# Attention scores as float32 products of 64 rows, two heads in the two row halves

## The chip, the cores and the metric

The kernel runs on one core of a Trainium2 chip. The metric is the device time of one execution in microseconds (us). The engines are TensorE (PE in the rows, PEld for its weight loads), VectorE (DVE), ScalarE (ACT), GpSimd (POOL) and SyncE (SP), which issues most of the DMAs.

## What is computed

A batch of one sequence of 512 tokens goes through two blocks in float32. The first block has two layers, each a hybrid mixer and a SwiGLU feed-forward. The mixer holds three kinds of heads side by side: attention with a sliding window, hgrn (a gated recurrence in chunks) and gdn (a delta rule in chunks). The second block has an even layer (attention over 512 own and 256 context tokens beside a two-directional mLSTM), a mixture of experts, an odd layer of window means, and again a mixture of experts. The scores of the two attentions are what the change is about:

```python
def sliding_window_attention(q, k, v, sinks):       # 8 query heads, 2 key heads of 64
    ...
    scores = jnp.einsum('bnqhgd,bnkhd->bnhgqk', qb, kb).astype(jnp.float32) * (d ** -0.5)
    ...                                             # 128 queries against 256 keys at a time
    m = jnp.maximum(scores.max(axis=-1, keepdims=True), sink)
    p = jnp.exp(scores - m)
...
def attend_blocks(q, k, v):                         # 8 query heads, 2 key heads, 768 keys
    ...
        s = jnp.einsum('bhgtd,bhsd->bhgts', qblk, kt).astype(jnp.float32) * scale
        p = jax.nn.softmax(s, axis=-1).astype(vt.dtype)
        return jnp.einsum('bhgts,bhsd->bhgtd', p, vt)
```

Four query heads share one key head. A head has 64 elements, so a score product sums over 64 rows of an array that has 128.

## The kernel before

All of it is one program on one core. The stages follow each other: layer 0 (stage "a0", then its feed-forward), layer 1, the even layer (stage "b"), experts, odd layer, experts. In a stage, pieces of work are written as Python generators that `mix` and `track` interleave; the order in which instructions then stand on each engine is set by a scheduler that runs over a simulated timeline (L2229). Tiles come from rotating pools, so a buffer's reuse is a wait. PSUM has eight banks of 128 x 512 float32, divided by name: in the layers two each for "pd", "pg", "po" and "ph", in the even stage two "pd", one "po", one "pn" and four "pe".

**Layers.** gdn is `gen_gdn` (banks "pg"), hgrn `gen_hgrn` (banks "ph"), attention `gen_attn` (L1251, banks "pd" and "po"). Queries ("aq", in the even stage "eqt") and keys and values ("kv") are projected with tokens in the partitions, normalized per head and rotated (the rope). To be multiplied, a head must be turned so that its 64 elements lie in the partitions. `stacked` (L1236) does that for one head, for each of four blocks of 128 tokens with two instructions: a transpose (`tr`) into rows 0 to 63 of a bank and a float32 product with the identity (`mm`) into rows 64 to 127. A float32 product appears as two records on TensorE.

`qstack` (L1244) turns that bank into a stack: ScalarE rounds it to the type F32R, GpSimd copies the rounded upper half, and DVE subtracts the rounded lower half from the exact one. So one stack holds a head's rounded queries in rows 0 to 63 and the rest in rows 64 to 127. Keys are split in the same way into a rounded part and a rest (`split`), each in both halves. One head's scores are then two F32R products of 128 rows, with the rounded keys and with their rest:

```python
                    self.mm(p[:, hh, k0:], Q, KS[:, h // 4, 0, K], True, False)
                    self.mm(p[:, hh, k0:], Q, KS[:, h // 4, 1, K], False, True)
```

In the layers `scores` goes over four blocks of 128 queries and four head pairs. A head pair shares one "pd" bank, DVE adds the mask and takes the maximum, ScalarE takes Exp into "sm". `gen_values` then transposes the weights (into "pg", from there to "PT") and multiplies with the values into "po"; the next block's scores run beside it.

**Even stage** (`even`, L1522). The same with `kstack` (L1389) for 512 own keys and 256 context keys (KSc, made early, between the input projections). `stack` inside it runs behind `rope`, beside the mLSTM (banks "pe", output projection through "pn"). In `scores` a head pair's own scores take two "pe" banks and its context scores, both heads side by side, one more. DVE reduces each of the three banks to its maximum, ScalarE takes four Exps ("eP"). "X" is the name of all large tiles (four buffers, `big`): hidden states, query stacks and key stacks.

Of the kernel before, what the change touches and what calls it, by code (L numbers as in the profile page):

```python
# [9 lines left out]
F32 = mybir.dt.float32  # L10
F32R = mybir.dt.float32r
I32 = mybir.dt.int32
AF = mybir.ActivationFunctionType
# [155 lines left out]
class Net:  # L169
# [1065 lines left out]

    def stacked(self, src, nb, tag="pd"):  # L1236

        p = self.psm(tag)
        for b in range(nb):
            self.tr(p[0:64, b * 128:b * 128 + 128], src(b))  # L1240
            self.mm(p[64:128, b * 128:b * 128 + 128], src(b), self.C("ident"))
        return p[:, :nb * 128]

    def qstack(self, QS, p):  # L1244

        tmp = self.t([128, 512], "qtmp", F32R)
        self.act(tmp, p)
        self.nc.gpsimd.tensor_copy(QS[0:64], tmp[0:64].bitcast(F32))
        self.tt(QS[64:128], p[64:128], tmp[64:128].bitcast(F32), OP.subtract)

    def gen_attn(self, l, qts, kv, out, banks):  # L1251
# [18 lines left out]
        for b in range(4):  # L1270
# [25 lines left out]
        def scores(b, keys):  # L1296
            k0 = 0 if b else 128
            K = slice(b * 128 - 128 + k0, b * 128 + 128)
            nm, den = self.t([128, 8], "nm"), self.t([128, 8], "den")
            P = []  # L1300
            for h2 in range(4):
                p = self.psm("pd").rearrange("p (h s) -> p h s", h=2)
                sm = self.t([128, 2, 256], "sm")
                hs = slice(2 * h2, 2 * h2 + 2)
                for hh in range(2):
                    h = 2 * h2 + hh
                    Q = QS[h // 4][:, h % 4, b * 128:b * 128 + 128]
                    self.mm(p[:, hh, k0:], Q, KS[:, h // 4, 0, K], True, False)
                    self.mm(p[:, hh, k0:], Q, KS[:, h // 4, 1, K], False, True)
                    nc.vector.tensor_tensor_reduce(sm[:, hh, k0:], p[:, hh, k0:], self.C("amask")[:, k0:], 1.0,  # L1310
                                                   self.P(f"sink{l}")[:, h:h + 1], OP.add, OP.max, nm[:, h:h + 1])
                self.ts(nm[:, hs], nm[:, hs], -1.0, OP.mult)
                for hh in range(2):
                    h = 2 * h2 + hh
                    x = sm[:, hh, k0:]
                    self.act(x, x, AF.Exp, bias=nm[:, h:h + 1], accum_out=den[:, h:h + 1])
                    P.append(sm[:, hh])
                yield
# [70 lines left out]
    def kstack(self, KS, kv, nb):  # L1389
        for i in range(2):  # L1390
            p = self.stacked(lambda b: kv[:, b, i * 64:i * 64 + 64], nb, "pd")
            self.split(p, KS[:, i, 0], KS[:, i, 1])

# [128 lines left out]
    def even(self, X, Xc, out, project):  # L1522
# [70 lines left out]

        stacks = []

        def rope():
# [15 lines left out]

        def stack():
            KS = self.big([128, 2, 2, 512], F32R)
            self.kstack(KS, kv, 4)
            yield
            QS = [self.big([128, 4, 512], F32R) for i in range(2)]
            stacks.extend([KS, QS])
            for h in range(8):
                self.qstack(QS[h // 4][:, h % 4], self.stacked(lambda b: qt[:, b, h * 64:h * 64 + 64], 4))  # L1620
                yield

        A = lambda g: self.track(g, "A", "pd")
        pk()
        self.run(pq(0), pq(1), silu(0), silu(1))
        self.run(self.mix((chain(ml(0), ml(2)), 1), (chain(iter([0, 0]), ml(1), ml(3)), 1), (chain(po(0), po(1), A(chain(pa(0), pa(1), rope(), stack()))), 3)))
        self.grp, self.pg = "A", "pd"
        KS, QS = stacks
        ao = [self.t([128, 512], "ao", grp="E") for j in range(4)]
        def scores(b, keys):  # L1630
            nm, den = self.t([128, 8], "nm"), self.t([128, 2, 8], "den")
            P, Pc = [], []
            for h2 in range(4):
                G = h2 // 2
                m3 = self.t([128, 2, 2], "em3")
                Q = [QS[G][:, (2 * h2 + hh) % 4, b * 128:b * 128 + 128] for hh in range(2)]
                pc = self.psm("pe").rearrange("p (h s) -> p h s", h=2)
                pl = []
                for hh in range(2):
# [5 lines left out]
                for hh in range(2):  # L1645
                    self.mm(pc[:, hh], Q[hh], self.KSc[:, G, 0], True, False)
                    self.mm(pc[:, hh], Q[hh], self.KSc[:, G, 1], False, True)
                nc.vector.tensor_reduce(m3[:, 1], pc, AX.X, OP.max)
                hs = slice(2 * h2, 2 * h2 + 2)
                self.tt(nm[:, hs], m3[:, 0], m3[:, 1], OP.max)  # L1650
                self.ts(nm[:, hs], nm[:, hs], -1.0, OP.mult)
                for hh in range(2):
                    h = 2 * h2 + hh
                    P.append(self.t([128, 512], "eP", grp="E"))
                    Pc.append(self.t([128, 256], "eP", grp="E"))
                    self.act(P[h], pl[hh], AF.Exp, bias=nm[:, h:h + 1], accum_out=den[:, 0, h:h + 1])
                    self.act(Pc[h], pc[:, hh], AF.Exp, bias=nm[:, h:h + 1], accum_out=den[:, 1, h:h + 1])
                yield
# [393 lines left out]
def build(nc, tc, a, cwhere, pwhere):  # L2052
    with ExitStack() as ctx:
# [20 lines left out]
        for l in range(2):  # L2074
            with ExitStack() as st:
                n.open(st, f"a{l}", {"G0": 11, "G1": 4, "G2": 20, "P2": 8, "I0": 1, "I1": 1, "I2": 8, "A0": 6, "A1": 3, "A2": 10, "B2": 2},
                       {"pd": 2, "pg": 2, "po": 2, "ph": 2})
# [70 lines left out]
        with ExitStack() as st:  # L2148
# [6 lines left out]
            m = n.m  # L2155
            n.KSc = m.tile([128, 2, 2, 256], F32R, name="KSc")
            n.V = m.tile([128, 6, 128], F32, name="V")
# [75 lines left out]
```

## Time and profile before

| | us |
|---|---|
| median of 3 runs | 3138.05 |
| lowest, highest | 3137.93, 3151.81 |
| the profiled execution | 3138.86 |
| its span, first to last instruction | 3137.1 |
| TensorE busy | 2956.0 (94%) |
| DVE busy | 1442.7 (46%) |
| ScalarE busy | 896.7 (29%) |
| GpSimd busy | 375.9 (12%) |
| mean share of the DMA engines | 56% (q1) |

The profile is one execution. Its chain view begins at the last instruction and goes back from each piece of work to what released it, so its shares tell which engine's work set the end. A window view gives for a stretch of time how long each engine was busy in it, the mean clock that TensorE was granted (1.00 is 2.4 GHz, 0.5 is 1.2 GHz) and what the DMA engines did. A timeline lists the records of one engine, like neighbours joined into one row with their count. A TensorE record's own length overlaps the next one's start, since products are pipelined; what a group takes from the engine is the distance from its start to the next group's start.

### The profile page before, as it was taken

To read this page: it belongs to the slowest core of one execution; us is meant where nothing else is said; L and a number is where in the kernel's file an instruction comes from. 1 tells how busy PE (TensorE), PEld (TensorE's weight loads), DVE (VectorE), ACT (ScalarE), POOL (GpSimd) and SP (SyncE) were. 2 spreads that over 40 slices of the span, in tenths; PEclk is the share of its full clock that TensorE was granted. 3 is DMA by queue.
4 is the path that set the end of the run, shared out by engine and by line. 5 is a ranking of instruction groups with operands and counts; after the bars stand their busy time and mean duration, and the time that the engine had idled before them with its cause. 6 is when DMAs were issued, how large, how long until landed. Compare 5 with 4: busy or idle time off the path is not lost.

```text
span 3137.1 us, 42862 instructions
## 1 busy us (share of the span) xinstructions
PE 2956.0 (94%) x17699; PEld 1982.9 (63%) x17699; DVE 1442.7 (46%) x2704; ACT 896.7 (29%) x1714; POOL 375.9 (12%) x308
## 2 busy tenths in 40 slices
PE   7999899999999899999999899899999988999998
PEld 5875678888886667888898855534444384344343
DVE  4345766564546658689545654411211362111112
ACT  4332443233432344423344434301101122011011
POOL 0212211011023202213100310100000021000000
PEclk9996899999999699999999989899999998999998
DMA  6233146563220016599512100699999828999995
GB/s 216 68 135 106 35 143 181 176 188 88 90 68 12 1 58 209 149 293 313 151 57 68 34 14 14 252 405 409 409 409 409 312 82 342 409 390 397 407 409 214
DMA packets 334403, 637.02 MB, mean 203 GB/s; under 512 B 16640, under 2 KB 204288, under 8 KB 334208
## 3 DMA queue, kind: packets, MB, share of 16 engines
q1 hardware_dynamic: 332128, 634.15, 55.9%
q8 instruction: 139, 2.28, 0.3%
q10 hardware_dynamic: 2080, 0.13, 0.0%
q14 instruction: 56, 0.46, 0.0%
HBM read 632.14 MB, written 2.10 MB: 202 GB/s over the span
## 4 chain that ended last, share of the span: by engine, by line
PE 85%; DVE 9%; ACT 2%; DMA 2%; issue 1%; POOL 0%; SPq 0%; DVEq 0%; POOLq 0%; ACTq 0%
PE pd L297 41%; PE pm L297 18%; PE pa L297 8%; PE po L297 4%; PE pg L297 4%; PE pe L297 3%; PE pd L301 3%; PE ph L297 2%; DVE aacc L294 1%; PE pn L297 1%; DVE x L294 1%; DMA raw<-ada_w 1%; PE pg L301 1%; DVE split L285 1%; DVE rt L285 1%
## 5 line engine op out<-in xcount | busy, mean ns | idle before, releaser
L297 PE MATMUL pd<-X,split 128*128 128x512 f32 x2640 | 629.7, 394 | 11.5 <-ACT X L274 6.8
L297 PEld LDWEIGHTS pd<-X,split 128*128 128x128 f32 x2640 | 493.2, 189 | 121.6 <-ACT X L274 10.0
L297 PE MATMUL pm<-rawx,xs 128*64 128x512 f32 x1440 | 403.7, 602 | 0.9 <-ACT xs L274 0.5
L297 PEld LDWEIGHTS pm<-rawx,xs 128*64 128x64 f32 x1440 | 126.2, 137 | 191.1 <-issue 181.9
L297 PE MATMUL pa<-rawx,maT 128*64 128x512 f32 x728 | 203.1, 601 | 7.6 <-ACT maT L274 7.6
L274 ACT ACTIVATE split<-raw 128x1024 fp32r<-128x1024 f32 (+5 forms) x164 | 142.0, 871 | 194.9 <-PE pd L297 130.9
L285 DVE TENSOR_TENSOR split<-raw,split 128x1024 fp32r<-128x1024 f32 (+4 forms) x135 | 150.5, 1120 | 89.5 <-ACT split L274 88.8
L297 PE MATMUL pd<-split,X 128*128 128x256 f32 x1296 | 179.0, 292 | 9.5 <-ACT split L274 5.8
L297 PEld LDWEIGHTS pd<-split,X 128*128 128x128 f32 x1296 | 164.6, 195 | 16.1 <-ACT split L274 5.9
L297 PE MATMUL pd<-X,splitx 128*128 128x512 f32 x720 | 173.6, 391 | 0.0
L297 PEld LDWEIGHTS pd<-X,splitx 128*128 128x128 f32 x720 | 135.6, 189 | 29.3
L297 PE MATMUL pd<-aH,split 128*128 128x512 f32 x484 | 153.4, 389 | 0.0
L294 DVE SCALAR_TENSOR_TENSOR x<-pd,modl,x 128x512 f32<-128x512 f32 x136 | 96.6, 746 | 98.1 <-PE pd L297 98.0
L294 DVE SCALAR_TENSOR_TENSOR yL<-pa,gv,yH 128x512 fp32r<-128x512 f32 x32 | 24.0, 751 | 245.9 <-ACT yH L274 245.9
L297 PEld LDWEIGHTS pa<-rawx,maT 128*64 128x64 f32 x728 | 67.4, 137 | 107.5 <-issue 95.9
L1985 DVE COPY gv<-pd 64x1 f32<-64x1 f32 x32 | 5.0, 156 | 273.8 <-PE pd L297 273.5
L285 DVE TENSOR_TENSOR ms<-ms,pm 128x512 f32<-128x512 f32 x32 | 22.0, 688 | 226.9 <-issue 186.9
L294 DVE SCALAR_TENSOR_TENSOR aacc<-rawx,cs_c,aacc 128x512 f32<-128x512 f32 x148 | 125.4, 889 | 0.0
L285 POOL TENSOR_TENSOR aL<-sg,aH 128x512 fp32r<-128x512 f32 x44 | 66.9, 1520 | 399.6 <-ACT aH L274 399.6
L297 PEld LDWEIGHTS pd<-aH,split 128*128 128x128 f32 x484 | 90.9, 188 | 19.3
L274 ACT ACTIVATE split<-rawx 128x1024 fp32r<-128x1024 f32 (+3 forms) x64 | 59.6, 934 | 151.6 <-PE pd L297 126.2
L297 PE MATMUL pm<-raw,xs 128*64 128x512 f32 x272 | 101.5, 597 | 0.0
(694 smaller groups left out, 4868.3 us busy)
## 6 DMA issues: line engine op xcount, KB each, us to landing
rawx<-w_exp_gate SPq DMA_DIRECT2D x94, 1024.0 KB, 15.9
rawx<-w_exp_down SPq DMA_DIRECT2D x91, 1024.0 KB, 12.5
rawx<-w_exp_up SPq DMA_DIRECT2D x86, 1024.0 KB, 18.0
raw<-ada_w SPq DMA_DIRECT2D x30, 1024.0 KB, 5.4
rawx<-w_mod SPq DMA_DIRECT2D x29, 1024.0 KB, 5.7
raw<-w_in SPq DMA_DIRECT2D x22, 1024.0 KB, 5.1
raw<-w_exp_up SPq DMA_DIRECT2D x20, 1024.0 KB, 16.9
raw<-w_mod SPq DMA_DIRECT2D x19, 1024.0 KB, 5.8
```

The costliest lines, as they stand in the source:

```text
L274: i = self.nc.scalar.activation(out, in_, f, **k)
L285: return (eng or self.nc.vector).tensor_tensor(out, a, b, op)
L294: return self.nc.vector.scalar_tensor_tensor(out, a, s, b, op0, op1)
L297: return self.nc.tensor.matmul(out, l, r, start=start, stop=stop, skip_group_check=True)
L301: return self.nc.tensor.transpose(out, x, self.C("ident")[0:k, 0:k])
L1985: nc.vector.tensor_copy(gv[64 * i:64 * i + 64], pg[64 * i:64 * i + 64, i:i + 1])
```

## The change

The stacks go. Instead of one head per transposition, two neighbouring heads (128 columns of the projected queries) are transposed at once: `gen_heads` makes four groups of four transposes, each 128 x 128, and ScalarE copies each group to a tile QT, head 2m in rows 0 to 63 and head 2m+1 in rows 64 to 127. For the keys, `twice` first has ScalarE copy each key head twice side by side ("kk"), so that the transposed key head (KT) lies in both halves. A head's scores are then one plain float32 product of 64 rows; the two heads of a pair are issued one after the other, from the two row halves and into two different banks.

In the layers this holds both "pd" banks for two head pairs. In the even stage a head pair takes all four "pe" banks, two for the own and two for the context scores, and DVE reduces four pieces instead of three. Rounding, the copies on GpSimd and the subtractions on DVE fall away, and KSc is half as large. The pool "A1" of the layers gets a fourth buffer.

```diff
-    def stacked(self, src, nb, tag="pd"):
-
-        p = self.psm(tag)
+    def twice(self, kv, nb, KT, tag="pd"):
+
+        kk = []
         for b in range(nb):
-            self.tr(p[0:64, b * 128:b * 128 + 128], src(b))
-            self.mm(p[64:128, b * 128:b * 128 + 128], src(b), self.C("ident"))
-        return p[:, :nb * 128]
-
-    def qstack(self, QS, p):
-
-        tmp = self.t([128, 512], "qtmp", F32R)
-        self.act(tmp, p)
-        self.nc.gpsimd.tensor_copy(QS[0:64], tmp[0:64].bitcast(F32))
-        self.tt(QS[64:128], p[64:128], tmp[64:128].bitcast(F32), OP.subtract)
+            t = self.t([128, 2, 2, 64], "kk")
+            self.act(t, self.bc1(kv[:, b, 0:128].rearrange("p (h e) -> p h e", h=2), 2))
+            kk.append(t.rearrange("p h i e -> p h (i e)"))
+        for i in range(2):
+            p = self.psm(tag)
+            for b in range(nb):
+                self.tr(p[:, b * 128:b * 128 + 128], kk[b][:, i])
+            self.act(KT[:, i], p[:, :nb * 128])
+            yield
+
+    def gen_heads(self, qt, kv, nb, tag="pd"):
+
+        QT, KT = self.big([128, 4, 512]), self.big([128, 2, 512])
+        self.stacks = KT, QT
+        yield from self.twice(kv, nb, KT, tag)
+        for m in range(4):
+            p = self.psm(tag)
+            for b in range(4):
+                self.tr(p[:, b * 128:b * 128 + 128], qt[:, b, m * 128:m * 128 + 128])
+            self.act(QT[:, m], p)
+            yield
...
-        KS = self.big([128, 2, 2, 512], F32R)
-        for i in range(2):
-            p = self.stacked(lambda b: kv[:, b, i * 64:i * 64 + 64], 4)
-            self.split(p, KS[:, i, 0], KS[:, i, 1])
-            yield
-        QS = [self.big([128, 4, 512], F32R) for i in range(2)]
-        for h in range(8):
-            self.qstack(QS[h // 4][:, h % 4], self.stacked(lambda b: qt[:, b, h * 64:h * 64 + 64], 4))
-            yield
+        yield from self.gen_heads(qt, kv, 4)
+        KT, QT = self.stacks
...
-            for h2 in range(4):
-                p = self.psm("pd").rearrange("p (h s) -> p h s", h=2)
...
-                    self.mm(p[:, hh, k0:], Q, KS[:, h // 4, 0, K], True, False)
-                    self.mm(p[:, hh, k0:], Q, KS[:, h // 4, 1, K], False, True)
...
+            for G in range(2):
+
+                pp = [self.psm("pd").rearrange("p (m s) -> p m s", m=2) for hh in range(2)]
+                for m in range(2):
+                    sm = self.t([128, 2, 256], "sm")
+                    h2 = 2 * G + m
+                    hs = slice(2 * h2, 2 * h2 + 2)
+                    for hh in range(2):
+                        r = slice(hh * 64, hh * 64 + 64)
+                        self.mm(pp[hh][:, m, k0:], QT[r, h2, b * 128:b * 128 + 128], KT[r, G, K])
...
-        self.kstack(self.KSc, Pair(kv.t[4:]), 2)
+        self.run(self.twice(Pair(kv.t[4:]), 2, self.KSc))
...
-                pc = self.psm("pe").rearrange("p (h s) -> p h s", h=2)
-                pl = []
-                for hh in range(2):
-                    p = self.psm("pe")
-                    self.mm(p, Q[hh], KS[:, G, 0], True, False)
-                    self.mm(p, Q[hh], KS[:, G, 1], False, True)
-                    nc.vector.tensor_reduce(m3[:, 0, hh:hh + 1], p, AX.X, OP.max)
-                    pl.append(p)
-                for hh in range(2):
-                    self.mm(pc[:, hh], Q[hh], self.KSc[:, G, 0], True, False)
-                    self.mm(pc[:, hh], Q[hh], self.KSc[:, G, 1], False, True)
-                nc.vector.tensor_reduce(m3[:, 1], pc, AX.X, OP.max)
+
+                pl, pc = [], []
+                half = [slice(hh * 64, hh * 64 + 64) for hh in range(2)]
+                for r in half:
+                    pl.append(self.psm("pe"))
+                    self.mm(pl[-1], QT[r, h2, b * 128:b * 128 + 128], KT[r, G])
+                for r in half:
+                    pc.append(self.psm("pe")[:, 0:256])
+                    self.mm(pc[-1], QT[r, h2, b * 128:b * 128 + 128], self.KSc[r, G])
+                for i, x in enumerate((pl, pc)):
+                    for hh in range(2):
+                        nc.vector.tensor_reduce(m3[:, i, hh:hh + 1], x[hh], AX.X, OP.max)
...
```

The scheduler then sets another order. The first place is TensorE in the even stage, where the first scores stand. Names: cst_g is the identity, eqt the queries of one token block, pd the bank of one group, pe the score banks, pn and eo the mLSTM's output projection. Before, in a row:

```order
L297 MATMUL pd_15576<-cst_g_60,eqt_13913 64x128
L301 MATMUL pd_15576<-cst_g_60,eqt_13914 64x128
L297 MATMUL pd_15576<-cst_g_60,eqt_13914 64x128
L301 MATMUL pd_15576<-cst_g_60,eqt_13915 64x128
L297 MATMUL pd_15576<-cst_g_60,eqt_13915 64x128
L297 MATMUL pn_15699<-eo_15607,split_15696 128x512
L297 MATMUL pn_15699<-eo_15608,split_15696 128x512
L297 MATMUL pn_15699<-eo_15607,split_15696 128x512
L297 MATMUL pe_15671<-X_15501,X_15524 128x512 x2
L301 MATMUL pd_15589<-cst_g_60,eqt_13912 64x128
L297 MATMUL pd_15589<-cst_g_60,eqt_13912 64x128
```

And now, in the same place:

```order
L297 MATMUL pn_15382<-eo_15338,split_15379 128x512
L301 MATMUL pd_15327<-cst_g_60,eqt_13680 128x128
L301 MATMUL pd_15327<-cst_g_60,eqt_13681 128x128
L301 MATMUL pd_15327<-cst_g_60,eqt_13682 128x128
L301 MATMUL pd_15327<-cst_g_60,eqt_13683 128x128
L297 MATMUL pe_15355<-X_15270,X_15269 128x512
L297 MATMUL pe_15357<-X_15270,X_15269 128x512
L297 MATMUL pe_15359<-KSc_12838,X_15269 128x256
L297 MATMUL pe_15361<-KSc_12838,X_15269 128x256
L301 MATMUL pd_15342<-cst_g_60,eqt_13680 128x128
L301 MATMUL pd_15342<-cst_g_60,eqt_13681 128x128
```

Four transposes stand where eight instructions a head stood, and the first pair's four products stand together between two groups.

The second place is TensorE in layer 0, in the scores of the last query block. pd are score banks, pg and sm the transposes of the weights, PT, kv and po the products with the values, rden the reciprocal sums. Before, in a row:

```order
L297 MATMUL pd_3129<-X_2604,X_2628 128x256 x2
L297 MATMUL pd_3140<-X_2604,X_2628 128x256 x2
L301 MATMUL pg_3172<-cst_g_60,sm_3092 128x128 x2
L297 MATMUL pd_3129<-X_2604,X_2628 128x256 x2
L297 MATMUL po_3153<-cst_g_60,rden_3151 64x128 x8
L301 MATMUL pg_3172<-cst_g_60,sm_3103 128x128
L297 MATMUL pd_3140<-X_2604,X_2628 128x256 x2
L301 MATMUL pg_3172<-cst_g_60,sm_3103 128x128
```

And now:

```order
L297 MATMUL pd_3018<-X_2605,X_2604 128x256
L301 MATMUL pg_3057<-cst_g_60,sm_2962 128x128 x2
L297 MATMUL po_2941<-PT_2996,kv_320 64x512
L297 MATMUL po_2941<-PT_3003,kv_320 64x512
L297 MATMUL pd_3019<-X_2605,X_2604 128x256
L297 MATMUL po_3038<-cst_g_60,rden_3036 64x128 x8
L301 MATMUL pg_3057<-cst_g_60,sm_2983 128x128
L297 MATMUL pd_3018<-X_2605,X_2604 128x256
L301 MATMUL pg_3057<-cst_g_60,sm_2983 128x128
L297 MATMUL pd_3019<-X_2605,X_2604 128x256
```

Before, a head's two products stood together. Now one product each of pd_3018 and pd_3019 is a head pair, and between the two halves of a pair other work was put.

## Rows read from the trace of the kernel before

**Rows 1.** The page's fourth part: the chain that ended last, by engine.

```profile
PE 85%; DVE 9%; ACT 2%; DMA 2%; issue 1%; POOL 0%; SPq 0%; DVEq 0%; POOLq 0%; ACTq 0%
```

**Rows 2.** Windows: stretch, length, busy us of PE, PEld, DVE, ACT, POOL, clock, DMA.

```profile
280.00:310.00 30.00, 29.75 (x199) 18.08 (x195) 9.30 (x27) 4.35 (x9) 3.65 (x6) 0.57 0.02 8
...
987.85:1024.50 36.65, 36.65 (x431) 23.36 (x429) 18.68 (x39) 11.40 (x21) 9.01 (x13) 1.00 0.03 9
1030.00:1060.00 30.00, 24.30 (x325) 20.35 (x324) 20.71 (x71) 11.86 (x31) 3.08 (x4) 0.53 0.01 2
...
1835.00:1967.00 132.00, 129.23 (x598) 69.75 (x598) 63.23 (x138) 59.90 (x168) 11.30 (x11) 1.00 0.05 17
```

**Rows 3.** Timeline of TensorE, even stage: start, length, line, out<-in, records.

```profile
1815.00 0.42 PE L301 MATMUL pd<-cst_g,eqt 128*64 128x128 f32 x1 [0.44 <-DVE X L285]
...
1818.89 1.12 PE L301 MATMUL pe<-cst_g,hm 128*128 128x128 f32 x4
1819.80 0.42 PE L301 MATMUL pd<-cst_g,eqt 128*64 128x128 f32 x1
...
1838.64 0.27 PE L301 MATMUL pd<-cst_g,eqt 128*64 128x128 f32 x1
...
1840.98 0.73 PE L297 MATMUL pe<-X 128*128 128x512 f32 x2
```

**Rows 4.** Timeline of TensorE, even stage, scores beside the block before's values.

```profile
1869.81 0.71 PE L297 MATMUL pe<-X 128*128 128x512 f32 x2
1870.45 1.07 PE L297 MATMUL po<-PT,V 128*64 128x512 f32 x2
1871.45 0.66 PE L301 MATMUL pd<-cst_g,eP 128*128 128x128 f32 x4
1871.86 0.72 PE L297 MATMUL pe<-KSc,X 128*128 128x256 f32 x4
...
1872.97 1.07 PE L297 MATMUL po<-PT,V 128*64 128x512 f32 x2
...
1877.57 0.71 PE L297 MATMUL pe<-X 128*128 128x512 f32 x2
```

**Rows 5.** Timeline of TensorE, layer 0: hgrn's 64-row products (ph).

```profile
360.90 0.61 PE L297 MATMUL ph<-ed 64*64 64x64 f32 x10
361.44 0.33 PE L301 MATMUL pg<-cst_g,sm 128*128 128x128 f32 x1
361.70 0.32 PE L297 MATMUL ph<-ed 64*64 64x64 f32 x2
361.96 0.33 PE L301 MATMUL pg<-cst_g,sm 128*128 128x128 f32 x1
362.22 0.33 PE L297 MATMUL ph<-ed 64*64 64x64 f32 x4
362.48 0.50 PE L297 MATMUL po<-zH,split 128*128 128x512 f32 x1
```

**Rows 6.** Timeline of TensorE, layer 0: a head pair's scores.

```profile
347.38 0.64 PE L297 MATMUL pd<-X 128*128 128x256 f32 x4
347.94 0.65 PE L297 MATMUL ph<-ed 64*64 64x32 f32 x14
```

**Rows 7.** Chain of waits, layer 0, 283 to 308 us: start, length, what.

```profile
284.39 0.62 PE pd L297 x2
...
305.05 0.31 PE pg L297 x2
...
306.63 0.14 DVE hO L285
```

**Rows 8.** Timeline of ScalarE, even stage: the Exps of one head pair.

```profile
1875.16 0.68 ACT L274 ACTIVATE eP<-pe,nm 128x512 f32<-128x512 f32 x1
...
1877.30 0.22 ACT L274 ACTIVATION_READ_ACCUMULATOR eP<-pe,nm 128x1 f32 x1
```

**Rows 9.** Timeline of SyncE: DMA issues behind the even stage.

```profile
1975.95 7.36 SPq L329 DMA_DIRECT2D rawx<-w_exp_gate  x8
```

More of the change, by code (lines that the diff above doesn't have):

```diff
@@ L1300, in scores @@
             P = []
-            for h2 in range(4):
-                p = self.psm("pd").rearrange("p (h s) -> p h s", h=2)
-                sm = self.t([128, 2, 256], "sm")
-                hs = slice(2 * h2, 2 * h2 + 2)
-                for hh in range(2):
-                    h = 2 * h2 + hh
-                    Q = QS[h // 4][:, h % 4, b * 128:b * 128 + 128]
-                    self.mm(p[:, hh, k0:], Q, KS[:, h // 4, 0, K], True, False)
-                    self.mm(p[:, hh, k0:], Q, KS[:, h // 4, 1, K], False, True)
-                    nc.vector.tensor_tensor_reduce(sm[:, hh, k0:], p[:, hh, k0:], self.C("amask")[:, k0:], 1.0,
-                                                   self.P(f"sink{l}")[:, h:h + 1], OP.add, OP.max, nm[:, h:h + 1])
-                self.ts(nm[:, hs], nm[:, hs], -1.0, OP.mult)
-                for hh in range(2):
[L1314 to L1318, printed above, removed]
+            for G in range(2):
[8 more added lines that the diff above has]
+                    for hh in range(2):
+                        h = 2 * h2 + hh
+                        nc.vector.tensor_tensor_reduce(sm[:, hh, k0:], pp[hh][:, m, k0:], self.C("amask")[:, k0:], 1.0,
+                                                       self.P(f"sink{l}")[:, h:h + 1], OP.add, OP.max, nm[:, h:h + 1])
+                    self.ts(nm[:, hs], nm[:, hs], -1.0, OP.mult)
+                    for hh in range(2):
+                        h = 2 * h2 + hh
+                        x = sm[:, hh, k0:]
+                        self.act(x, x, AF.Exp, bias=nm[:, h:h + 1], accum_out=den[:, h:h + 1])
+                        P.append(sm[:, hh])
+                    yield
             self.tt(nm, nm, self.P(f"sink{l}"), OP.add)
@@ L1387, in ssq @@
         self.nc.vector.tensor_reduce(dst, sq.rearrange("p (h e) -> p h e", e=64), AX.X, OP.add)
[L1389 to L1392, printed above, removed]
     def conv3(self, c, p, n, dst, silu=True):
@@ L1611, in rope @@
                 yield
[L1613 to L1621, printed above, removed]
         A = lambda g: self.track(g, "A", "pd")
@@ L1625, in even @@
         self.run(pq(0), pq(1), silu(0), silu(1))
-        self.run(self.mix((chain(ml(0), ml(2)), 1), (chain(iter([0, 0]), ml(1), ml(3)), 1), (chain(po(0), po(1), A(chain(pa(0), pa(1), rope(), stack()))), 3)))
+        self.run(self.mix((chain(ml(0), ml(2)), 1), (chain(iter([0, 0]), ml(1), ml(3)), 1), (chain(po(0), po(1), A(chain(pa(0), pa(1), rope(), self.gen_heads(qt, kv, 4)))), 3)))
         self.grp, self.pg = "A", "pd"
-        KS, QS = stacks
+        KT, QT = self.stacks
         ao = [self.t([128, 512], "ao", grp="E") for j in range(4)]
@@ L1635, in scores @@
                 m3 = self.t([128, 2, 2], "em3")
[L1636 to L1648 removed]
+                pl, pc = [], []
[7 more added lines that the diff above has]
+                for i, x in enumerate((pl, pc)):
+                    for hh in range(2):
+                        nc.vector.tensor_reduce(m3[:, i, hh:hh + 1], x[hh], AX.X, OP.max)
                 hs = slice(2 * h2, 2 * h2 + 2)
@@ L1656, in scores @@
                     self.act(P[h], pl[hh], AF.Exp, bias=nm[:, h:h + 1], accum_out=den[:, 0, h:h + 1])
-                    self.act(Pc[h], pc[:, hh], AF.Exp, bias=nm[:, h:h + 1], accum_out=den[:, 1, h:h + 1])
+                    self.act(Pc[h], pc[hh], AF.Exp, bias=nm[:, h:h + 1], accum_out=den[:, 1, h:h + 1])
                 yield
@@ L2075, in build @@
             with ExitStack() as st:
-                n.open(st, f"a{l}", {"G0": 11, "G1": 4, "G2": 20, "P2": 8, "I0": 1, "I1": 1, "I2": 8, "A0": 6, "A1": 3, "A2": 10, "B2": 2},
+                n.open(st, f"a{l}", {"G0": 11, "G1": 4, "G2": 20, "P2": 8, "I0": 1, "I1": 1, "I2": 8, "A0": 6, "A1": 4, "A2": 10, "B2": 2},
                        {"pd": 2, "pg": 2, "po": 2, "ph": 2})
@@ L2155, in build @@
             m = n.m
-            n.KSc = m.tile([128, 2, 2, 256], F32R, name="KSc")
+            n.KSc = m.tile([128, 2, 256], F32, name="KSc")
             n.V = m.tile([128, 6, 128], F32, name="V")
```

1 line of the change is left out of this document (removed).

## The prediction

> **What bounds the kernel now.** First the chain of work that ended last [rows 1]: TensorE holds 85% of it, DVE 9%, everything else a few per cent. So an edit counts by what it takes from TensorE's queue, and only where TensorE is what the stage waits for. That is read stage by stage from the busy time in windows [rows 2]. Attention has its transposes and scores in three places. In layer 0, from 280 to 310 us, TensorE is busy 29.75 of 30 us at a granted clock of 0.57. In layer 1, from 987.85 to 1024.50, it is busy without a gap at 1.00. In the even stage, from 1835 to 1967, it is busy 129.2 of 132 us at 1.00. What follows each place is a dense block of TensorE work that starts when the mixer's result is there, and the expert weights are issued only behind the even stage's output (SyncE's first w_exp_gate issue stands at 1975.95) [rows 9], so I let a shift pass to the end undiminished. The profiled run took 3138.86 us (3137.1 of it span), 0.8 above the median of 3138.05.
>
> **Transposes removed.** Before, each of 8 query heads and 2 key heads takes four pieces of one transpose and one float32 product with the identity (two records). In the even stage one head takes 3.89 us at the low clock (1815.00 to 1818.89) and 2.34 at the high (1838.64 to 1840.98) [rows 3]. After, two heads go together in four plain transposes. Rows show that form: four 128x128 transposes take 0.91 at the low clock (1818.89 to 1819.80) [rows 3] and 0.41 at the high (1871.45 to 1871.86) [rows 4].
> Even stage: three heads at the low clock and five at the high, 3 x 3.89 + 5 x 2.34 = 23.4, become 4 x 0.91 = 3.6 (all at the low clock, the dearer end): **-19.8**. The first place in the order shows it: between two groups there stand four transposes where eight instructions for each head stood. All of it lies behind the rope, with nothing else for TensorE to do there but the mLSTM's projection, which comes later either way.
> The two context key groups, inside the dense input projection: 2 x 2 pieces of 2.34/4 become two visits of some 0.3 each, **-1.7** (nothing, if the projection waits there for something else).
> Layer 0: five heads' transposes lie behind the last ada row, from 284.39 to 305.05 [rows 7], 5 x 3.89 = 19.5; two and a half new groups take 2.3: -17.2. The heads ahead of 283 lie beside the wait for ada_w and count nothing.
> Layer 1: all ten groups lie in the gapless window from 987.85, which begins with the first key piece [rows 2], 10 x 2.34 = 23.4; six new groups at 0.41 and 0.16 for coming and going (below) take 3.4: -20.0.
> Copies and casts: eight casts on ScalarE and GpSimd and eight subtractions on DVE go, six ScalarE copies of a bank and four of doubled keys come. In the chain they stood behind the last head alone; no gain is counted for them.
>
> **Scores changed, even stage.** Before, a head pair costs what its rows show [rows 4]: 0.64 for two 512-column products, then 1.11 for four 256-column and two 512-column ones (1871.86 to 1872.97): 1.75, or 16 x 1.75 = 28.0. After, it is two float32 products of 512 columns from rows 0-63 and 64-127, and two of 256. A float32 product is two records. Two of 512 columns on 128 rows take 1.00 in the trace (1870.45 to 1871.45, two records: one product) [rows 4]. Whether two row halves run side by side is shown by hgrn: one 64-row product alone holds TensorE 0.26 (361.70 to 361.96), a pair from the two halves 0.26 as well (362.22 to 362.48) [rows 5]. So an adjacent pair costs about one product. Ten such records in a stream take 0.54 (360.90 to 361.44) [rows 5], so of a lone visit 0.11 is its two records and some 0.16 is coming and going, an estimate. A 512 pair then costs 1.02, a 256 pair 0.43 + 0.16 = 0.60; pairs between which the scheduler puts other work cost twice that. The order of the changed kernel has 13 adjacent and 3 split 512 pairs, and 12 and 4 of 256: 13 x 1.02 + 3 x 2.04 + 12 x 0.60 + 4 x 1.20 = 31.4. **+3.4**.
>
> **Scores changed, layers.** A head pair's four rounded 256-column products take 0.56 (347.38 to 347.94) [rows 6]. An adjacent float32 pair costs 0.59, a split one 1.18. In layer 0 two of twelve 256-column pairs are adjacent and ten split, the second place in the order: 10 x 0.62 + 2 x 0.03 = +6.3. In layer 1 five and seven: +4.5. The 128-column ones of block 0 I set at nothing (within +-2, by the same rows).
>
> **Banks.** A head pair of the even stage now holds all four score banks until its last Exp; before it held three. Its chain is products 1.6, then maxima and negation 2.2 (products left at 1872.97, first Exp at 1875.16), then the Exps to 1877.52 [rows 8]: 6.2 us. A pair comes around every 7.8 (1869.81 to 1877.57) [rows 4], so TensorE's values and transposes hide it with 1.6 us to spare. If that cover is gone, each us over 7.8 costs up to 12 us (three blocks of four).
>
> **A page against this change.** The trace shows 0.16 us around each lone 64-row visit [rows 5]. The Trainium skill, page TensorEngine Tiling (Array Packing), section Key Properties, says that changing the tiling mode drains the TensorE; by that rule every visit of scores of 64 rows, some 94 in the three stages, would pay it, and 94 x 0.16 = 15 us is an estimate of the whole. It is in the prices above; without it the sum would be some 15 us lower, 3082. The old scores were 128-row products and paid none.
>
> **Sum.** Even stage -19.8 - 1.7 + 3.4 = -18.1; layer 0 -17.2 + 6.3 = -10.9; layer 1 -20.0 + 4.5 = -15.5; together -44.5. In the two layers the delta-rule and hgrn chains run beside the transposes and have DVE steps between their small products; without the transposes TensorE will wait for some of these. Bounds for what is given back: nothing, and all 37 us. In 280 to 310 the rest of the work fills about 12 us of what would be 13, so I take 3 us. 3138.9 - 44.5 + 3 - 0.8 = **3097**.
>
> **The rivals.**
> Freed time hidden in the layers: the chains of gdn and hgrn set the end of this stretch and not the transposes. For it: in layer 1 TensorE is busy only 24.30 of 30 us right after, at 1030 to 1060 [rows 2]. Against it: no gap at all in the window before. All 37.2 are given back, while the split pairs stay: 3138 - 18.1 + 10.8 = 3131, within the bound of no change.
> Row halves run one after the other: the scheduler's order gives pairs side by side, yet the even pairs are products of 512 columns of two passes, and no row shows such a pair. Then 13 pairs pay 0.85 more and 12 pay 0.43, 16.2 in the even stage, 3.4 in the layers: 3097 + 20 = 3117.
> Cheaper visits: the 0.16 is paid seldom: 3082.
> Slower than before: the clock. In the even stage the records have the low clock's length at 1819.80 and the high one's at 1838.64, with transposes without a gap between [rows 3]. After the change these are gone and what follows is scores that wait for banks and Exps. Where TensorE has gaps the clock is low: 0.53 at 24.3 of 30 us [rows 2]. Were it to stay at 1.2 GHz (half of 2.4) through the even attention, each us of the 129 that is at 1.00 now takes up to one more: at worst 3097 + 116 = 3213 for the stretch from 1851 on. It decides from 42 us of such work on: fewer, and it eats only the gain. Against it: at 1864 to 1881, values and transposes follow each other almost without a gap at the high clock [rows 4], and they stay.
> That the change doesn't do what it says is excluded: the rows of the order are there.
>
> **How the numbers follow.** Forecast 0.57; cheaper visits 0.08; row halves in series 0.12; hidden in the layers 0.14; the clock 0.09. 0.5% of 3138, about what a measurement of this kernel can tell from no change, is 15.7 us: 3122 to 3154 is the same. Faster: 0.57 + 0.08 + 0.12 = 0.77; same: 0.14; slower: 0.09. The range takes in the cheaper visits with 6 us for the unpriced 128-column pairs and the layers' chains (3076), the serial halves (3117) and the hidden layers' case up to its middle (3131); the clock case lies outside.
>
> **What would show it.** Right: in the even stage the groups of four transposes follow the rope within 4 us and the window from rope to the first dense output block is some 17 us shorter; adjacent 512 pairs occupy about 1.0 us; layer 0's hO comes some 16 us earlier, at about 290 (306.63 before) [rows 7], and the mixers end 11 and 27 us earlier in all. Wrong: a pair of 512 that takes 1.9; gaps in TensorE's row behind DVE and ScalarE in the layers between 284 and 300; a clock of 0.5 to 0.7 in the even stage; pairs in the even stage more than 7.8 us apart with TensorE waiting for a bank.

## The result, and the profile after

The changed kernel takes 3103.48 us in the median of four runs (3089.32 to 3107.11); before, on the same chips, 3140.33. The ratio over these runs is 0.9874, with a 95% interval of 0.985 to 0.9899: faster by 1.26%; the two medians are 36.9 us apart. The prediction said 3097, between 3076 and 3131. The profiled execution took 3102.67 us, 3100.9 of it span.

The chain that ended last is made as before (page, fourth part; its row of before is [rows 1]):

```profile
PE 85%; DVE 9%; ACT 2%; issue 2%; DMA 1%; POOL 0%; DVEq 0%; POOLq 0%; ACTq 0%
```

To see where the time went, the span is cut at events that both traces have: the first dense product behind each mixer (pd<-X,split) and SyncE's first w_exp_gate issue.

| us | before | after | difference | predicted |
|---|---|---|---|---|
| start to end of layer 0's mixer | 399.54 | 390.59 | -9.0 | -10.9 |
| to end of layer 1's mixer | 751.36 | 733.30 | -18.1 | -15.5 |
| to the first w_exp_gate issue | 825.05 | 814.49 | -10.6 | -18.1 |
| the rest | 1161.15 | 1162.52 | +1.4 | 0 |
| sum | 3137.1 | 3100.9 | -36.2 | -44.5, 3 of it given back |

The even stage as TensorE saw it, first its beginning and then a steady piece (timeline: start, length, line, out<-in, records; answers to [rows 3, 4]):

```profile
1789.96 1.52 PE L301 MATMUL pd<-cst_g,eqt 128*128 128x128 f32 x8
1791.23 1.08 PE L297 MATMUL pn<-eo,split 128*128 128x512 f32 x3
1792.15 0.60 PE L301 MATMUL pd<-cst_g,eqt 128*128 128x128 f32 x4
1792.68 1.13 PE L297 MATMUL pe<-X 64*128 64x512 f32 x4
1793.64 0.60 PE L297 MATMUL pe<-KSc,X 64*128 64x256 f32 x4
1794.17 0.66 PE L301 MATMUL pd<-cst_g,eqt 128*128 128x128 f32 x4
...
1830.88 0.66 PE L301 MATMUL pd<-cst_g,eP 128*128 128x128 f32 x4
1831.46 1.13 PE L297 MATMUL pe<-X 64*128 64x512 f32 x4
1832.52 1.07 PE L297 MATMUL po<-PT,V 128*64 128x512 f32 x2
1833.53 0.66 PE L301 MATMUL pd<-cst_g,eP 128*128 128x128 f32 x4
1834.11 0.70 PE L297 MATMUL pe<-KSc,X 64*128 64x256 f32 x4
1834.75 1.07 PE L297 MATMUL po<-PT,V 128*64 128x512 f32 x2
```

All 16 query transposes of the stage pass between 1789.96 and 1794.59 with the first scores between them; before, eight heads needed from 1815.00 to 1850.48. A pair of 512-column products (four records) takes 1.06 from its start to the next work (1831.46 to 1832.52), a pair of 256 columns 0.64 (1834.11 to 1834.75). One more thing is in these rows: the four transposes ahead of either pair take 0.58 (1830.88 to 1831.46), and they took 0.41 ahead of the 128-row scores [rows 4].

The windows of layer 0 and of the even stage (stretch, length, busy time of PE, PEld, DVE, ACT, POOL, clock, DMA; answers to [rows 2]):

```profile
300.00:320.00 20.00, 14.60 (x212) 11.79 (x209) 16.73 (x40) 6.56 (x13) 6.91 (x8) 0.67 0.01 2
320.00:340.00 20.00, 20.00 (x119) 11.25 (x119) 9.03 (x35) 5.91 (x18) 1.70 (x2) 0.58 0.00 1
340.00:360.00 20.00, 19.79 (x142) 11.73 (x141) 8.68 (x28) 7.55 (x26) 2.91 (x4) 1.00 0.18 54
...
1789.96:1815.00 25.04, 24.76 (x112) 15.22 (x111) 13.75 (x31) 12.84 (x35) 5.09 (x4) 0.98 0.13 43
1815.00:1840.00 25.00, 24.67 (x93) 8.98 (x93) 10.91 (x25) 12.65 (x39) 1.26 (x1) 1.00 0.00 0
1840.00:1860.00 20.00, 18.86 (x78) 9.68 (x76) 10.24 (x26) 7.03 (x20) 1.27 (x1) 0.83 0.08 27
1860.00:1936.20 76.20, 74.00 (x330) 34.11 (x329) 32.28 (x79) 31.09 (x83) 2.54 (x2) 1.00 0.02 8
```

Two stretches stand out: in layer 0 TensorE is busy all of 320 to 340 and is granted only 0.58 there, and in the even stage 1840 to 1860 has idle time and 0.83. The latter begins with a wait for a score bank (timeline of TensorE):

```profile
1843.37 1.12 PE L297 MATMUL pe<-X 64*128 64x512 f32 x2 [1.14 <-ACT eP L274]
1844.42 0.33 PE L301 MATMUL pd<-cst_g,eP 128*128 128x128 f32 x1
1844.68 1.24 PE L297 MATMUL pe<-X 64*128 64x512 f32 x2
1845.85 1.11 PE L301 MATMUL pd<-cst_g,eP 128*128 128x128 f32 x4
1846.89 1.22 PE L297 MATMUL pe<-KSc,X 64*128 64x256 f32 x2
...
1849.60 4.29 PE L297 MATMUL pn<-eo,split 128*128 128x512 f32 x12
```

At a block's start TensorE waits 1.14 us for an Exp to give a bank back; behind that the records are the low clock's (four transposes 1.04, twelve products of the mLSTM's projection 4.29, and 3.04 at 1881.45). At 1853.82 it is over.

### The profile page after: what moved, and what is told of

Same layout as the page of the kernel before. It is cut to its first block, busy times and chain, and to the rows that moved or that the text cites. A ratio compares the mean times of both kernels' runs of the same rounds, so it can differ in the third digit from the quotient of the medians.

```text
span 3100.9 us, 42214 instructions
## 1 busy us (share of the span) xinstructions
PE 2921.0 (94%) x17403; PEld 1958.3 (63%) x17403; DVE 1422.8 (46%) x2688; ACT 894.8 (29%) x1716; POOL 361.4 (12%) x284
## 4 chain that ended last, share of the span: by engine, by line
PE 85%; DVE 9%; ACT 2%; issue 2%; DMA 1%; POOL 0%; DVEq 0%; POOLq 0%; ACTq 0%
PE pd L297 41%; PE pm L297 18%; PE pa L297 8%; PE po L297 4%; PE pg L297 4%; PE pe L297 3%; PE pd L301 2%; PE ph L297 2%; DVE aacc L294 1%; PE pn L297 1%; DVE x L294 1%; PE pg L301 1%; DMA raw<-ada_w 1%; DVE rt L285 1%; DVE split L285 1%
```

## The experiments

All kernels ran beside runs of the kernel before. Stage lengths are read at the same events as above, each from one profiled execution; where nothing was changed they still differ by a few us (behind the w_exp_gate issue 1160.65 in e_round and 1157.63 in e_round_early); "even" ends with the w_exp_gate issue, "turning" is the transposition of heads, "scores" the products. "Old" is the kernel before's way.

| us | turning | scores | median | ratio to before, 95% | layer 0 | layer 1 | even |
|---|---|---|---|---|---|---|---|
| before | old | old | | | 399.54 | 751.36 | 825.05 |
| after | new | 64 rows | 3103.48 | 0.9874 [0.985, 0.9899] | 390.59 | 733.30 | 814.49 |
| e_old_turn | old | 64 rows | 3155.21 | 1.0057 [1.0038, 1.0076] | 403.44 | 752.25 | 840.72 |
| e_old_scores | new | old, false data | 3078.46 | 0.9812 [0.9783, 0.9841] | 379.81 | 733.71 | 801.28 |
| e_round | new | old | 3088.24 | 0.9842 [0.9814, 0.987] | 378.61 | 737.09 | 806.75 |
| e_same_half | new | 64 rows, one half | 3125.07 | 0.9951 [0.993, 0.9971] | 395.19 | 743.36 | 825.73 |
| e_adj | new | 64 rows, pairs together | 3077.91 | 0.9811 [0.9785, 0.9837] | 370.27 | 726.83 | 816.24 |
| e_adj_exps | new | the same, Exps reordered | 3076.92 | 0.9802 [0.9782, 0.9822] | 369.82 | 726.80 | 813.89 |
| e_adj_qf | new, queries first | 64 rows, pairs together | 3072.60 | 0.9783 [0.9768, 0.9798] | 370.11 | 724.99 | 816.31 |
| e_round_early | new | old, written early | 3067.96 | 0.9767 [0.9751, 0.9784] | 368.36 | 732.50 | 806.21 |
| e_before_early | old | old, written early | 3139.69 | 0.9999 [0.9983, 1.0014] | 400.22 | 746.48 | 826.26 |

**Turning undone: e_old_turn.** The old `stacked` is back, one head at a time, for queries and both kinds of keys:

```diff
...
         for m in range(4):
-            p = self.psm(tag)
-            for b in range(4):
-                self.tr(p[:, b * 128:b * 128 + 128], qt[:, b, m * 128:m * 128 + 128])
-            self.act(QT[:, m], p)
-            yield
+            for hh in range(2):
+                h, r = 2 * m + hh, slice(hh * 64, hh * 64 + 64)
+                p = self.stacked(lambda b: qt[:, b, h * 64:h * 64 + 64], 4, tag)
+                self.act(QT[r, m], p[r])
+                yield
```

> The changed kernel, but heads are turned as before: one head at a time, a transpose into rows 0-63 and a product with the identity into rows 64-127, of which ScalarE copies the half that is wanted; keys and context keys too. Scores stay float32 products of 64 rows. Theory (the turning is the gain, the scores cost): the transposes come back with their 58 us, the scores keep their +14: about 3154, slower than before by some 14. Rival (the gain is the elementwise work of the stacks, the casts on GpSimd and subtractions on DVE, which stay away here): 3103 to 3115. In the even stage the window from the first query transposes to the output block should be 159 us plus 3 by the theory, 146 by the rival.

Measured 3155.21, slower than before by 0.57%: the theory's 3154. The elementwise work of the stacks stayed away in this kernel, so its absence is not what the gain came from. By stages the near hit is in part luck: against before, layer 0 is +3.9, layer 1 +0.9 and the even stage +15.7, where the prices of the scores are +6.3, +4.5 and +3.4, and the unchanged rest is 5.5 shorter. From the first query transpose to the output block the even stage took 175.7 us (1818.6 to 1994.3), 14 more than the theory's 162. The whole even stage is 26.2 us longer than after; the turning there runs without a gap at the low clock, 0.50 (window, columns as above):

```profile
1818.60:1845.00 26.40, 26.40 (x74) 11.15 (x73) 6.06 (x13) 4.19 (x7) 1.26 (x1) 0.50 0.00 0
```

**Scores undone: e_old_scores and e_round.** The first puts two rounded products of 128 rows a head on the tile that holds two heads (so the scores are of false data); the second makes the true rounded and rest parts from the two-head bank:

```diff
...
+            for hh in range(2):
+                h = 2 * m + hh
+                q, r, o = QS[h // 4][:, h % 4], slice(hh * 64, hh * 64 + 64), slice(64 - hh * 64, 128 - hh * 64)
+                self.act(q[r], p[r])
+                self.tt(q[o], p[r], q[r].bitcast(F32), OP.subtract)
...
```

> The changed kernel's transposes, but scores as two rounded products of 128 rows for each head, as many and as long as before (on the tile that holds two heads, so the values are not the scores; the rest term is computed from the same keys). Theory: before less 58 for the transposes, of which the layers and the even stage give back some 10: 3085 to 3092. Rival (the products of 64 rows are cheaper than I priced and carry part of the gain): 3110 or more.

> Two heads are turned at once as in the changed kernel, but then split again as before: ScalarE rounds each half bank, DVE subtracts it and writes the rest into the other half; scores are before's two rounded products of 128 rows a head, keys with rounded and rest part. The result is the reference's. Theory (the turning is the whole gain, 64-row scores cost 20 to 25): 3078 to 3085, level with the run that had rounded products on unsplit tiles (3078). Rival (the extra four half-bank pieces on ScalarE and DVE for each two heads hold up the first scores): 3090 or more.

3078.46 and 3088.24: both medians below the changed kernel's, the first under its range by 7 us, the second above its own by 3 and short of the rival's 3090. The interval of e_old_scores lies apart from the changed kernel's, that of e_round overlaps it. So, by the medians, the 64-row scores took back 15 to 25 us of what the turning gave. By stages, after against e_round: layer 0 +12.0, layer 1 -3.8, even +7.7. The 5.5 us between the two in the even stage come with the splitting into rounded part and rest: e_round's first score product waits for DVE ("0.26 <-DVE X" at 1785.51), and its TensorE waits 2.3 us for Exps, which it doesn't in e_old_scores. The rest of the 5.5 was not taken apart.

The even stage of e_old_scores shows the neighbours' price directly (timeline of TensorE):

```profile
1808.22 0.66 PE L301 MATMUL pd<-cst_g,eP 128*128 128x128 f32 x4
1808.63 0.71 PE L297 MATMUL pe<-X 128*128 128x512 f32 x2
1809.28 1.07 PE L297 MATMUL po<-PT,V 128*64 128x512 f32 x2
```

The same four transposes ahead of the same scores take 0.41 here and 0.58 in the changed kernel. So a visit of 64-row products costs 0.17 when it comes, and it costs something when it goes too (0.21, from e_same_half below). It is not peculiar to 64 rows. In the kernel before, the same transposes take 0.59 ahead of the values' products, which use 64 columns of the array ("128*64", rows*columns; timeline of TensorE):

```profile
1873.98 0.66 PE L301 MATMUL pd<-cst_g,eP 128*128 128x128 f32 x4
1874.57 1.07 PE L297 MATMUL po<-PT,V 128*64 128x512 f32 x2
```

Ahead of a float32 product of 128 rows and 128 columns (pe<-va,kw, 1706.98 to 1707.41) four transposes take 0.43. So what these rows charge is the change of form, in rows or in columns, and not the float32 product.

**One row half: e_same_half.** Both heads of a pair read rows 0-63, `r = slice(0, 64)`; the second head's scores are then false.

> The changed kernel, but both heads of a pair are read from rows 0-63 (the second head's scores are then the first's). Theory (two row halves run side by side, one half does not): 13 adjacent 512 pairs of the even stage cost 0.85 more and 12 of 256 0.43 more, 16 us, and the layers' 7 adjacent 256 pairs 0.43, 3 us: 3103 + 19 = 3122; the 512 pair takes 1.9 us from its start to the next work instead of 1.06. Rival (the records only look as if side by side, and each waits its turn anyway): 3103, a pair 1.06 to 1.3.

Measured 3125.07 against 3103.48 and an expected 3122. The same pair as above (timeline of TensorE):

```profile
1841.90 1.98 PE L297 MATMUL pe<-X 64*128 64x512 f32 x4
1843.81 1.07 PE L297 MATMUL po<-PT,V 128*64 128x512 f32 x2
...
1845.40 1.13 PE L297 MATMUL pe<-KSc,X 64*128 64x256 f32 x4
1846.46 1.07 PE L297 MATMUL po<-PT,V 128*64 128x512 f32 x2
```

1.91 and 1.06 from one half, 1.06 and 0.64 from two: two row halves do run side by side, and an adjacent pair costs one product. The second product of 512 columns adds 0.85, so of the pair's 1.06 some 0.21 is not the product. That the sum came near 3122 is in part luck: the even stage is 11.2 us longer where 16 were expected, the layers 14.7 where 3 were.

**Pairs put together: e_adj.** In the layers the four products of a bank pair are written ahead of their maxima; all 32 pairs of the two layers then stand together in the order.

```diff
                 for m in range(2):
+                    for hh in range(2):
+                        r = slice(hh * 64, hh * 64 + 64)
+                        self.mm(pp[hh][:, m, k0:], QT[r, 2 * G + m, b * 128:b * 128 + 128], KT[r, G, K])
+                for m in range(2):
                     sm = self.t([128, 2, 256], "sm")
...
-                    for hh in range(2):
-                        r = slice(hh * 64, hh * 64 + 64)
-                        self.mm(pp[hh][:, m, k0:], QT[r, h2, b * 128:b * 128 + 128], KT[r, G, K])
```

> The changed kernel, but in the layers the four products of a bank pair are written ahead of the four maxima, by which all 32 pairs of the layers stand together in the order (17 of 24 pairs of 256 and 6 of 8 of 128 columns were split). Theory (a split pair pays a second visit): 17 x 0.59 = 10 us less, 3093, the mixer of layer 0 some 6 and that of layer 1 some 4 us shorter. Rival (the split products are fill while gdn, hgrn or the Exps set the end): 3100 to 3106.

3077.91, 25.6 us less than the changed kernel where the theory had 10: layer 0 is 20.3 shorter, layer 1 6.5. The direction is the theory's, the size is not. In layer 0 the clock tells a part of it (windows of e_adj and, under it, of e_round; the changed kernel's own row for this stretch has 0.58):

```profile
320.00:340.00 20.00, 20.00 (x145) 12.23 (x141) 12.91 (x52) 10.88 (x36) 3.16 (x4) 0.94 0.04 14
```

```profile
320.00:340.00 20.00, 20.00 (x174) 12.75 (x173) 14.07 (x50) 9.12 (x26) 4.87 (x6) 0.93 0.05 15
```

All three are busy for the whole 20 us.

**Is it the visits or the order? e_round_early and e_before_early.** The same rewriting, products of two head pairs ahead of their maxima, for the rounded products of 128 rows, which have no visits to save: once with the new turning, once in the kernel before.

```diff
-                p = self.psm("pd").rearrange("p (h s) -> p h s", h=2)
+                if h2 % 2 == 0:
+                    pp = [self.psm("pd").rearrange("p (h s) -> p h s", h=2) for m in range(2)]
+                    for h in range(2 * h2, 2 * h2 + 4):
+                        Q = QS[h // 4][:, h % 4, b * 128:b * 128 + 128]
+                        o = pp[h // 2 % 2][:, h % 2, k0:]
+                        self.mm(o, Q, KS[:, h // 4, 0, K], True, False)
+                        self.mm(o, Q, KS[:, h // 4, 1, K], False, True)
+                p = pp[h2 % 2]
...
-                    Q = QS[h // 4][:, h % 4, b * 128:b * 128 + 128]
-                    self.mm(p[:, hh, k0:], Q, KS[:, h // 4, 0, K], True, False)
-                    self.mm(p[:, hh, k0:], Q, KS[:, h // 4, 1, K], False, True)
```

> The run before (two heads turned at once, rounded products of 128 rows), with the eight products of two head pairs written ahead of their maxima in the layers. It separates two readings of the 26 us that the same rewriting gave the 64-row products. By the visits (a lone 64-row product pays for changing over at both ends, and rounded products of 128 rows don't): within 5 us of the run without it. By the order (products ahead of maxima let TensorE run ahead whatever their rows): 15 us less in layer 0 and 10 in layer 1, about 3055.

> The kernel before, unchanged but for the layers' rounded products: the eight of two head pairs are written ahead of their four maxima. Theory (what the written order gave, 20 us beside the two-head transposes, doesn't depend on how heads are turned): 10 to 20 us less than before, most of it in layer 1. Rival (it is the shorter turning that lets TensorE come to the scores early enough for the order to matter): within 5 us of before.

With the new turning it gives 20.3 us (3088.24 to 3067.96), 10.3 of it in layer 0 and 4.6 in layer 1: neither the first reading's 5 nor the second's 25, but nearer the second. So of e_adj's 20.3 in layer 0 about half is the order, and so is 4.6 of its 6.5 in layer 1. What is left, 10.1 and 1.9, comes with the 64-row products alone: their split visits, and the clock, which is not separated from them. With both written early, the 64-row kernel (e_adj) is 3.8 us shorter in the two layers together than the rounded one (e_round_early) and 10.0 longer in the even stage: what the 64-row products still cost lies there.

In the kernel before, the rewriting is worth nothing (0.9999), so the theory of e_before_early falls and its rival holds. Its profile has layer 0 0.7 longer and layer 1 4.9 shorter, as much as with the new turning, which the median doesn't bear out. In layer 0, then, the order pays only with the new turning; for layer 1 the runs don't decide it.

**Queries first, Exps reordered: e_adj_qf and e_adj_exps.** In the first the call of `twice` is moved behind the loop over query groups; in the second both Exps of the own scores stand ahead of those of the context scores.

> The 64-row kernel with the layers' pairs together (3078), and the four query groups turned ahead of the two key groups, so that ScalarE's doubling of the keys runs beside them. Theory (in the even stage TensorE waited 5.2 us at 1786.50 and 0.6 at 1787.77 for those copies, of which some 2 are the copies' own): the even stage 2 us shorter, 3076, the layers unchanged. Rival (the rope's last piece is the key's, and the first scores need the keys anyway): no change, 3078.

> The 64-row kernel with the layers' pairs together (3078), and in the even stage both Exps of own scores ahead of both of context scores, so that a pair's two big banks come free together. Theory (the 1.14 us that TensorE waits for the first bank at a block's start and the low clock that follows it cost some 4 us): if the wait goes, 3074. Rival (the order now has 7 instead of 4 split context pairs, at 0.6 each, and the wait stays): 3078 to 3081.

3072.60 and 3076.92, neither apart from e_adj's 3077.91 by their intervals. Queries first leaves the even stage as it was, 816.31 to 816.24, so the key copies were not what held it up: TensorE now waits for DVE's rope of the queries instead (4.08 us at 1745.67, 2.44 at 1753.96). With the Exps reordered the stage is 2.4 us shorter, the wait at the block's start is 0.72 instead of 1.14, and the low clock behind it is gone (windows of e_adj_exps, then of e_adj):

```profile
1815.00:1835.00 20.00, 19.28 (x87) 9.12 (x85) 11.28 (x29) 9.48 (x28) 1.27 (x1) 1.00 0.09 27
```

```profile
1815.00:1835.00 20.00, 18.86 (x76) 9.70 (x76) 10.29 (x26) 7.03 (x20) 1.27 (x1) 0.83 0.08 26
```

A form with both heads' context scores in one bank was not run, so what the fourth bank costs by itself is not shown.

The fastest that was run is e_round_early, 0.9767 of before: the turning of the change with the scores of before, written early. Its interval just misses that of e_adj, the 64-row scores written early.

## Why the prediction came out as it did

**What bounds the kernel: right.** What the mixers' ends moved came off the end of the program; the rest of the program passed the shift on, with 1.4 us lost behind 1938.38, where the first gate issue now stands (timeline of SyncE; before [rows 9]):

```profile
1938.38 7.42 SPq L329 DMA_DIRECT2D rawx<-w_exp_gate  x8
```

**Transposes: right in sum, -58.7 predicted.** After against e_old_turn gives -51.2 in the span and e_round against before -54.0, with the splitting work of e_round in it. The clock is part of the first: e_old_turn's even stage has the low level until about 1853, that of before until about 1830. By stages (before to e_round) it is -20.9, -14.3 and -18.3, for -17.2, -20.0 and -21.5. In layer 0 the mechanism was a different one in part. The prediction let the transposes behind the last ada row go and counted those ahead of it as free. They were not: with half of them gone TensorE came to the ada rows 8.4 us earlier (their last product stands at 274.31 where it stood at 282.74), and no query transposes are left behind that point. hO is there at 283.30 (306.63 before, [rows 7]), 23 us earlier where 16 were named (timelines of TensorE and of DVE).

```profile
274.31 1.05 PE L297 MATMUL po<-cst_g,arow 128*128 128x2 f32 x8
```

```profile
283.30 0.69 DVE L285 TENSOR_TENSOR hO<-ph,dv 128x512 f32<-128x512 f32 x1 [0.42 <-PE ph L297]
```

All that the prediction priced lay behind that row, and there the changed kernel won nothing: from it to the mixer's end it takes 116.3 us (274.31 to 390.59), before 116.8 (282.74 to 399.54), and e_round 103.9 (274.76 to 378.61). So layer 0's -9.0, near the -10.9 of the sum, is luck: it is the 8.4 us of the heads that were set at nothing, while the 13 us that the turning gave behind the row went to the 64-row scores and the low clock that came with them. The sign that the prediction named for freed time that turns into waiting, gaps behind DVE between 284 and 300, did appear (3.3 us), but over the whole stretch TensorE's gaps hardly grew, 11.9 us for 11.0.

**An adjacent pair costs one product: right.** 1.02 and 0.60 were predicted, 1.06 and 0.64 measured; e_same_half shows what it would be otherwise.

**The even stage's scores: the term that was mis-sized.** +3.4 predicted; +7.7 against e_round, +13.2 against e_old_scores. What was too small is the price of a visit. Its 0.16 was taken once, for coming and going together; the trace charges the work ahead too (0.58 for 0.41). The prediction's own rows had it: one transpose ahead of a lone visit holds TensorE 0.26 (361.44 to 361.70, [rows 5]), where a quarter of 0.41 is 0.10. 35 visits stand in this stage, 31 of them behind work on 128 rows and 128 columns; 31 x 0.17 = 5.3 us is an estimate of what was left out.

The bank comes second. "TensorE's values and transposes hide it with 1.6 us to spare" holds inside a block (a pair comes around every 8.05 us, 1863.26 to 1871.31, and TensorE waits for nothing), but not at its start, where the values of the next block have not begun. That was so in the kernel before, with three banks (timeline of TensorE):

```profile
1862.56 0.73 PE L297 MATMUL pe<-X 128*128 128x512 f32 x2 [0.99 <-ACT eP L274]
```

In all, TensorE waited 1.3 us for Exps in this stage before, 2.0 in the changed kernel, 2.3 in e_round and not at all in e_old_scores. So the wait is no part of the +7.7 against e_round. The low clock behind it is: from 1844 to 1854 the changed kernel was granted 0.66, some 3.4 us lost by an estimate from that figure, where e_round has 1.00 throughout from its first scores (1785.51) on. Why the clock fell behind the wait of 1.14 and not behind the 0.99 before is not shown.

**The Trainium skill's drain: it agrees, and weighed more.** The Trainium skill, page TensorEngine Tiling (Array Packing), section Key Properties, has the change of tiling mode drain the TensorE. The prediction took it once per visit, 15 us. The rows show a price at both ends, 0.17 and some 0.21. That "the old scores were 128-row products and paid none" is true of their coming (0.41); the values behind them are a change of form too, and transposes ahead of those paid 0.17 in the kernel before (0.59, 1873.98 to 1874.57).

**The layers' scores: right in sum, wrong in place.** +6.3 and +4.5 predicted, +12.0 and -3.8 measured (after to e_round). Why the extra visits don't show in layer 1 was not isolated; TensorE has gaps of 16.8 us in all there between the first query transpose and the layer's end, 16.4 in e_round. In layer 0 they came with 22 us at the low clock (314 to 336).

**The rivals.** Row halves in series: ruled out (e_same_half). Gain hidden in the layers: not so in sum, they gave 27 of 36 us, though layer 0 gave none of it where the prediction had it. Cheaper visits: the opposite. The clock in the even stage: it did drop, within the 10 us from 1844 to 1854 and not for 116. In layer 0 it had its effect where the prediction did not look for it.

**What stays open.** Why the clock in layer 0 rises so late in the changed kernel was not isolated. TensorE counts as busy throughout from 314 us on, and the low level still lasts until about 337 (256-column pairs take 1.15 at 330.35 and 0.64 at 336.99; timeline of TensorE):

```profile
330.35 1.23 PE L297 MATMUL pd<-X 64*128 64x256 f32 x4
...
336.99 0.70 PE L297 MATMUL pd<-X 64*128 64x256 f32 x4
```

e_adj is at 0.50 from 312 to 321 and e_round from 312 to 322, also without a gap, and both then have the full clock (windows of the changed kernel, e_adj and e_round):

```profile
314.00:336.00 22.00, 22.00 (x150) 13.90 (x149) 11.04 (x39) 8.37 (x21) 2.91 (x3) 0.50 0.00 1
```

```profile
324.00:336.00 12.00, 12.00 (x93) 7.64 (x90) 7.98 (x31) 6.69 (x23) 1.47 (x2) 1.00 0.07 23
```

```profile
324.00:336.00 12.00, 12.00 (x104) 8.76 (x103) 8.82 (x32) 6.31 (x19) 2.45 (x3) 1.00 0.07 23
```

Some 14 us at half the clock are 7 us of work at the full one, an estimate: that much of layer 0's 12 us can be the clock. But e_adj changes the visits and the order at once, and e_round has neither visits nor split pairs, so whether the visits hold the clock down is not known.

## What to carry to other kernels

A change with two parts is worth undoing in halves: here turning two heads at once gave some 54 us, and the 64-row products that came with it gave 18 of them back, so the first part with the old products came out ahead of the whole (with both written early 3067.96 against 3077.91, intervals just apart; against the whole's best variant, 3072.60, they overlap). Two row halves of the array ran side by side at the price of one product where the order had them next to each other, and every separate visit was paid for at its ends: write such products in groups, ahead of what reads them. Where a resource looks covered in the steady piece, look at the block's first round too, in which the cover has not started yet; the kernel before already waited there. And a sum that comes out right can be made of parts that don't: read each stage from the event that the prediction named.

## What was not expected of the hardware

Four transposes took 0.17 us longer only by what stood behind them: 0.41 ahead of products on 128 rows and 128 columns, 0.58 ahead of products on 64 rows, and 0.59 ahead of products on 64 columns, in the kernel before too. So a visit's price stands partly in a row that the change doesn't touch. And TensorE was at a granted 0.50 over 22 us in which its record has no gap, where two kernels with fewer separate 64-row visits, or none, were at 1.00 from 324 us on.
